# A hybrid decoder step on one core: norms and projections interleaved, free PSUM banks first, and eight idle matmuls ahead of the data

## The chip, the cores and the metric

One NeuronCore of a Trainium2 chip runs the whole program. The metric is the device time of one execution in microseconds (us); the profile shows one execution. TensorE is "PE" in the profile (its weight loads are "PEld"), VectorE "DVE", ScalarE "ACT", GpSimd "POOL", SyncE "SP"; a "q" behind an engine's name is its queue of DMA issues.

## The reference

One layer over 16 meta tokens, a prompt of 2048 and 64 sample tokens (8 sequences of 8), model width 1024. Cut to its frame:

```python
def layer(x):                       # x: tokens x 1024
    q, k, v, c, vm, o, i, f = split(x @ w_in)          # 512 128 128 512 512 512 4 4
    att = window_attention(q, k, v)                    # window 128, sinks, ALiBi
    h_m = mlstm(silu(conv4(c)), vm, i, f)              # 4 heads of 128, chunks of 128
    y = concat(head_norm(att), head_norm(sigmoid(o) * h_m))
    x1 = layer_norm(ALPHA * x + y @ w_out, ln1)
    ffn = (silu(x1 @ w_gate) * (x1 @ w_up)) @ w_down   # inner width 2816
    return layer_norm(ALPHA * x1 + ffn, ln2)           # and the caches and states
```

Matrix products must come out at float32 accuracy.

## The kernel before

Every large product is done in three passes (`mm3`, L125 to L127): each float32 operand is split into a high part, rounded to the fast matmul type (a cast, L113 on ScalarE, L115 on GpSimd, L117 on VectorE), and a low part, the difference (L122, on VectorE, now and then on GpSimd), and high x high, high x low and low x high are added up in PSUM. So each weight tile or activation tile that is loaded costs a DMA, a cast and a subtraction ahead of its first matmul.

A planner writes out the order of each engine's instructions when the kernel is built: it takes the instructions by their place in the Python code, and passes over those that are not ready by its own clock. On the chip every engine then keeps that order. `tc.issue_after(ins)` adds an edge: what is traced inside it on the engine of `ins` is put behind `ins` in that engine's order.

PSUM has two pools of banks: `pg` with three (`gps()`), `pb` with five (`bps()`).

The stages:

- First phase (to about 255 us): token tiles of 128 are projected onto v, the gates, vm and o with `w1a`. Tiles 0 and 1 run together, weight slice by weight slice as it arrives (`load_w1`), tile 0 in `gps`, tile 1 in `bps` banks. From tile 2 on each takes three banks in turn, from `gps` or `bps` by a counter `flip`. A tile's PSUM is emptied by VectorE and ScalarE (L273 to L298). `load_x` makes raw, high and low of a tile in buffers that share a tag. At the loop's thirteenth tile the code loads the first weights (`load_w`, one raw buffer `wbr`) and the first columns of x (`load_xg`) of the next phase; the planner hoists these.
- Second phase: q, k, c, the convolution and the maps of the mLSTM, by five groups of columns; the last group's three last projections (`late`) are left for the third phase.
- Third phase: five groups `g` of 384 to 440 tokens. For each: `out_proj` (eight steps `m` of 24 matmuls, each ended by the eviction L1091, ALPHA * z + projection), the layer norm `ln1`, gate and up (`gate_up`), and `down` in four slices, each of eight steps `m` ended by L1271. Attention and mLSTM of later tokens run between as background steps (`bg_step`, `pace`). `wnext` hands out weight tiles and loads three ahead.

The norms are Python generators; each `yield` gives the code around a place to put other work. `norm` (groups 1 to 4, and `ln2`): the mean by a matmul with `avg` (L1104), subtraction (L1108), squares (L1110), their sums (L1115), sums over partitions by matmuls (L453), 1/std on VectorE (`rsqrt`, L131 to L138) and its broadcast by matmuls (L465). `norm_early` (the first group's `ln1`, and the last group's `ln2_tail`) takes a provisional mean of the first four rows of tiles (`avg4`, L1128) while the rest is still being projected, and corrects it at the end: squares L1135, sums L1139, matmuls L1166 to L1171, 1/std, broadcast L1184. Then `scale` (L1205) multiplies, and ScalarE adds the bias (L1199 in the tail, L1214 and L1223 in `ln1`, whose low halves are L1221 on VectorE and L1224 on GpSimd).

The generators are stepped from outside: in the last slice of `down`, `ln1` of the next group is stepped twice at m = 0 and once at m = 1, 4 and 5; the tail's norm from m = 4 on; and in the first group `out_proj` steps it from m = 4 on, and the loop around `out_proj` runs it to its end before the `late` projections:

```python
        for _ in out_proj(z, y0, FF_GROUPS[0], lambda s: ln1(z, FF_GROUPS[0], s, x1, True, mark)):
            pass
        for m in late:
```

Of the kernel before, what the change touches and what calls it, by code (L numbers as in the profile page):

```python
# [16 lines left out]
D = 1024  # L17
# [27 lines left out]
CZ = 3  # L45

# [3 lines left out]
def tile_hymba(  # L50
# [42 lines left out]
    def constants():  # L93
        SP.dma_start(out=C, in_=cst)
        SP.dma_start(out=Q, in_=par)
        SP.dma_start(out=R, in_=rows.to_broadcast([128, 16]))
        V.memset(avg, 1.0 / D)
        V.memset(avg4, 2.0 / D)
        V.memset(one1, 1.0)
        V.tensor_copy(blk, C[:, C_BD:C_BD + 128])  # L100
# [40 lines left out]
    flip = [0]  # L141
# [43 lines left out]
    with ExitStack() as s1:  # L185
# [3 lines left out]
        def load_x(cols, parts=((0, KD),), eng="a"):  # L189
            raw = xp.tile([128, KD, 128], F32, tag="x", name="xr", bufs=6)  # L190
            hi = xp.tile([128, KD, 128], F32R, tag="x", name="xh", bufs=6)
            lo = xp.tile([128, KD, 128], F32R, tag="x", name="xl", bufs=6)
# [33 lines left out]

        x0, x1 = (load_x(tiles[i], ((0, 2), (2, KD)), "v") for i in range(2))
# [18 lines left out]
        for i in range(NCH + 1):  # L246
            if i == NCH - 4:
                with tc.issue_after(w1dma[0].ins):
                    for j in range(NEARLY):
                        load_w(j)  # L250
                    for k in range(KD):
                        load_xg(0, k)
# [45 lines left out]
            A.activation(out=o[0:n, 128:512], in_=pc[0:n, 0:384], func=AF.Tanh, scale=0.5)  # L298
# [712 lines left out]
    with ExitStack() as s2:  # L1011
# [34 lines left out]
        def wnext():  # L1046
            while len(ahead) < 3:
                t = next(wit, None)
                ahead.append(None if t is None else wtile(*t))
            return ahead.pop(0)  # L1050
# [33 lines left out]
        def out_proj(z, y, w, ln=None):  # L1084
            s = fp.tile([128, FW], F32, tag="zs", name="zs", bufs=2)
            for m in range(KD):
                h, l = wnext()
                p = gps()
                for k in range(KD):
                    mm3(p[:, 0:w], h[:, k, :], l[:, k, :], y[k][0][:, 0:w], y[k][1][:, 0:w], k == 0, k == KD - 1)  # L1090
                V.scalar_tensor_tensor(out=z[m][:, 0:w], in0=z[m][:, 0:w], scalar=ALPHA, in1=p[:, 0:w],  # L1091
                                       op0=ALU.mult, op1=ALU.add)
# [29 lines left out]
        def norm_early(z, w, s, pre):  # L1122
# [5 lines left out]
            PE.matmul(cm[:, 0:w], lhsT=avg4, rhs=s[:, 0:w], start=True, stop=True)  # L1128
            for k in (5, 6, 7):
# [30 lines left out]
            t = square(7)  # L1160
            parts = 3 if w % 3 == 0 and w <= 384 else 4
# [26 lines left out]
        def ln2_tail(z, g, s, w):  # L1188
            c0 = sum(FF_GROUPS[:g])
            ry = yield from norm_early(z, w, s, 1.0)  # L1190
            rs = ftmp()
            A.copy(rs[:, 0:w], ry[:, 0:w])
            for k in (6, 0, 1, 2, 7, 3, 4, 5):
                if k > 5:
                    G.tensor_tensor(out=z[k][:, 0:w], in0=z[k][:, 0:w], in1=rs[:, 0:w], op=ALU.mult)
                else:
                    scale(z, k, w, ry, Q_L2G)
            for k in (0, 1, 2, 6, 3, 4, 7, 5):
                A.activation(out=z[k][:, 0:w], in_=z[k][:, 0:w], func=AF.Identity, bias=Q[:, Q_L2B + k:Q_L2B + k + 1],  # L1199
                             scale=Q[:, Q_L2G + k:Q_L2G + k + 1] if k > 5 else 1.0)  # L1200
# [91 lines left out]
        for _ in out_proj(z, y0, FF_GROUPS[0], lambda s: ln1(z, FF_GROUPS[0], s, x1, True, mark)):  # L1292
            pass
        for m in late:
# [4 lines left out]
            out_q(None, p, m, cl, wl_)  # L1299
        ready[0] = T  # L1300
# [7 lines left out]
        for g in range(NG):  # L1308
# [4 lines left out]
            for s, n in enumerate(SLICES):  # L1313
# [21 lines left out]
                for m, _ in enumerate(down(z, hs, s, w, zs, 4 if last else KD)):  # L1335
                    if ln is not None and m in (0, 1, 4, 5):
# [3 lines left out]
                    if last and zs is not None and m >= 4:  # L1340
                        if m == 4:
# [130 lines left out]
```

## Time and profile before

| | us |
|---|---|
| median of 3 runs | 2491.41 |
| lowest and highest | 2490.56, 2494.92 |
| the profiled execution, its time | 2488.45 |
| its span on the core | 2486.7 |
| PE busy in it | 2438.5 |
| mean granted clock of PE | 0.993 |

A row of a timeline is: start, duration, engine, line, operation, output<-inputs, shape, count (merged rows), and in brackets the idle time before it and what ended that. A row of the stretches is: from:to, length, then busy time (and count) of PE, PEld, DVE, ACT, POOL, then PE's granted clock, the DMA share and GB/s. A matmul's duration holds its way through the array; matmuls in a row start closer together than they last. A row that begins with a line number gives minimum, median and maximum duration in ns and the first and last start.

### The profile page before, as it was taken

To read this page: it belongs to the slowest core of one execution; us is meant where nothing else is said; L and a number is where in the kernel's file an instruction comes from. 1 tells how busy PE (TensorE), PEld (TensorE's weight loads), DVE (VectorE), ACT (ScalarE), POOL (GpSimd) and SP (SyncE) were. 2 spreads that over 40 slices of the span, in tenths; PEclk is the share of its full clock that TensorE was granted. 3 is DMA by queue.
4 is the path that set the end of the run, shared out by engine and by line. 5 is a ranking of instruction groups with operands and counts; after the bars stand their busy time and mean duration, and the time that the engine had idled before them with its cause. 6 is when DMAs were issued, how large, how long until landed. Compare 5 with 4: busy or idle time off the path is not lost.

```text
span 2486.7 us, 35083 instructions
## 1 busy us (share of the span) xinstructions
PE 2438.5 (98%) x13189; PEld 2273.0 (91%) x13189; DVE 1535.3 (62%) x3195; ACT 965.3 (39%) x1752; POOL 311.6 (13%) x241
## 2 busy tenths in 40 slices
PE   8999999989999999999999999999999999999997
PEld 8999989889999998889999899989899999999997
DVE  5223577677877877757665886666765444764445
ACT  3112455545434445324443543343443323443332
POOL 1000000010000015110003300000410000420000
PEclk9999999999999999999999999999999999999998
DMA  7222534554444543554443354433344333343342
GB/s 236 91 91 76 174 117 127 171 174 139 152 139 127 170 135 110 181 153 136 127 132 116 118 182 122 139 113 116 102 143 130 120 111 119 102 145 113 119 127 78
DMA packets 188867, 327.89 MB, mean 132 GB/s; under 512 B 22546, under 2 KB 125034, under 8 KB 188682
## 3 DMA queue, kind: packets, MB, share of 16 engines
q1 hardware_dynamic: 170832, 294.40, 38.7%
q10 hardware_dynamic: 17866, 31.26, 3.4%
q8 instruction: 104, 1.70, 0.3%
q14 instruction: 65, 0.53, 0.1%
HBM read 281.59 MB, written 44.99 MB: 131 GB/s over the span
## 4 chain that ended last, share of the span: by engine, by line
PE 90%; DVE 4%; DMA 3%; ACT 1%; issue 1%; POOL 0%; ACTq 0%; SPq 0%; DVEq 0%; POOLq 0%
PE gps L125 25%; PE gps L126 25%; PE gps L127 25%; PE bps L125 2%; PE bps L127 2%; PE bps L126 2%; PE bps L516 2%; PE bps L552 1%; PE bps L545 1%; DVE w L122 1%; PE bps L658 1%; PE bps L685 1%; PE bps L675 1%; DMA w<-in_wd 1%; DMA w<-in_wg 1%
## 5 line engine op out<-in xcount | busy, mean ns | idle before, releaser
L127 PE MATMUL gps<-x,w 128*128 128x440 f32 (+4 forms) x2240 | 795.8, 356 | 4.3 <-POOL w L122 2.2
L126 PE MATMUL gps<-x,w 128*128 128x440 f32 (+4 forms) x2240 | 795.3, 356 | 0.0
L125 PE MATMUL gps<-x,w 128*128 128x440 f32 (+4 forms) x2240 | 790.0, 357 | 2.9 <-DVE z L1091 2.9
L113 ACT CAST w<-w 128x1024 fp32r<-128x1024 f32 (+2 forms) x423 | 400.5, 947 | 749.8 <-DMA w<-in_wd 261.1
L122 DVE TENSOR_TENSOR w<-w 128x1024 fp32r<-128x1024 f32 (+2 forms) x391 | 443.0, 1133 | 352.9 <-ACT w L113 163.7
L125 PEld LDWEIGHTS gps<-x,w 128*128 128x128 f32 x2240 | 420.5, 188 | 30.4 <-issue 5.4
L127 PEld LDWEIGHTS gps<-x,w 128*128 128x128 f32 x2240 | 420.9, 188 | 22.9 <-POOL w L122 3.7
L126 PEld LDWEIGHTS gps<-x,w 128*128 128x128 f32 x2240 | 421.1, 188 | 17.6 <-issue 0.2
L125 PE MATMUL gps<-hh,w 128*128 128x440 f32 (+2 forms) x880 | 314.6, 361 | 0.0
L127 PE MATMUL gps<-hh,w 128*128 128x440 f32 (+2 forms) x880 | 313.6, 358 | 0.0
L126 PE MATMUL gps<-hl,w 128*128 128x440 f32 (+2 forms) x880 | 312.9, 357 | 0.0
L122 POOL TENSOR_TENSOR w<-w 128x1024 fp32r<-128x1024 f32 x32 | 78.2, 2444 | 852.1 <-ACT w L113 611.5
L126 PEld LDWEIGHTS gps<-hl,w 128*128 128x128 f32 x880 | 166.5, 189 | 8.8 <-issue 2.3
L125 PEld LDWEIGHTS gps<-hh,w 128*128 128x128 f32 x880 | 166.1, 189 | 8.7 <-issue 1.7
L127 PEld LDWEIGHTS gps<-hh,w 128*128 128x128 f32 x880 | 166.2, 189 | 8.2 <-issue 1.1
L1271 DVE SCALAR_TENSOR_TENSOR z<-z,gps 128x440 f32<-128x440 f32 (+2 forms) x160 | 92.9, 589 | 57.7 <-PE gps L127 56.8
L113 ACT CAST hh<-hr 128x440 fp32r<-128x440 f32 (+2 forms) x110 | 60.0, 545 | 155.0 <-DVE hr L1257 154.9
L1257 DVE SCALAR_TENSOR_TENSOR hr<-ft,gps 128x440 f32<-128x440 f32 (+2 forms) x110 | 64.9, 590 | 81.7 <-PE gps L127 81.2
L1254 ACT ACTIVATE ft<-gps 128x440 f32<-128x440 f32 (+2 forms) x110 | 57.3, 521 | 106.3 <-PE gps L127 106.0
L122 DVE TENSOR_TENSOR hl<-hr,hh 128x440 fp32r<-128x440 f32 (+2 forms) x110 | 78.3, 712 | 27.2 <-ACT hh L113 26.7
L1255 DVE SCALAR_TENSOR_TENSOR ft<-ft,gps 128x440 f32<-128x440 f32 (+2 forms) x110 | 64.6, 588 | 39.5 <-ACT ft L1254 39.3
L126 PE MATMUL bps<-w1l,xh 128*128 128x384 f32 (+2 forms) x240 | 81.5, 339 | 0.0
(370 smaller groups left out, 3158.8 us busy)
## 6 DMA issues: line engine op xcount, KB each, us to landing
w<-in_wg SPq DMA_DIRECT2D x110, 512.0 KB, 3.5
w<-in_wu SPq DMA_DIRECT2D x110, 512.0 KB, 3.5
w<-in_wd SPq DMA_DIRECT2D x80, 384.0 KB, 3.1
w<-in_wd SPq DMA_DIRECT2D x80, 320.0 KB, 2.9
w<-in_wo SPq DMA_DIRECT2D x40, 512.0 KB, 3.7
FM<-ev ACTq DMA_DIRECT2D x52, 213.0 KB, 2.1
TM<-st ACTq DMA_DIRECT2D x16, 578.0 KB, 3.7
vmo<-TM SPq DMA_DIRECT2D x16, 514.0 KB, 3.5
```

The costliest lines, as they stand in the source:

```text
L113: A.copy(out, src)
L122: return veng.tensor_tensor(out=lo, in0=src, in1=hi.bitcast(F32), op=ALU.subtract)
L125: PE.matmul(out, lhsT=wh, rhs=xh, start=start, stop=False)
L126: PE.matmul(out, lhsT=wh, rhs=xl, start=False, stop=False)
L127: PE.matmul(out, lhsT=wl, rhs=xh, start=False, stop=stop)
L516: PE.matmul(s[g][:, j, 0:nk], lhsT=x[r, 2 * tt + j, :], rhs=y[r, 0:nk], start=(i == 0), stop=(i == 2))
L545: PE.transpose(pt[0:n, 128 * t:128 * t + 128], Pt[:, 4 * g + t, c0:c0 + n], ident)
L552: mm = PE.matmul(o[64 * g:64 * g + 64, :], lhsT=vt[0:n, j, 64 * g:64 * g + 64], rhs=ps[g][0:n], start=(j == 0), stop=(j == 1), skip_group_ ...
L1254: A.activation(out=t[:, 0:w], in_=pgt[:, 0:w], func=AF.Tanh, scale=0.5)
L1255: V.scalar_tensor_tensor(out=t[:, 0:w], in0=t[:, 0:w], scalar=1.0, in1=pgt[:, 0:w], op0=ALU.add, op1=ALU.mult)
L1257: V.scalar_tensor_tensor(out=hr[:, 0:w], in0=t[:, 0:w], scalar=0.5, in1=pu[:, 0:w], op0=ALU.mult, op1=ALU.mult)
L1271: V.scalar_tensor_tensor(out=zm, in0=zm, scalar=ALPHA if s == 0 else 1.0, in1=p[:, 0:w], op0=ALU.mult, op1=ALU.add)
```

## The change

- The memsets of `avg` and `avg4` move ahead of all loads, and eight matmuls of 128x128 on them are put into a bank that nothing reads (`WARM`).
- `flip` starts at 3, so tile 2 takes its three banks from `pb` first.
- `load_x` has seven buffers in place of six.
- The early `load_w` and `load_xg` get a second edge: their ScalarE work is put behind `evict`, ScalarE's last eviction of tile 1.
- `wnext(ins)`: in `out_proj` the splits of a tile that is newly loaded go behind the previous step's eviction on VectorE.
- `out_proj` starts `ln1` of the first group at m = 3 in place of 4; `norm_early` has three more yields (after the provisional mean, before the sums over partitions, before the broadcast); and the rest of that norm is stepped between the three `late` projections.
- The later `ln1` is stepped at m = 0, 0, 1, 3, 5 in place of 0, 0, 1, 4, 5; the tail's norm from m = 3 in place of 4.
- `ln2_tail` scales all eight tiles on VectorE and sends them in order; the copy of 1/std by ScalarE and two multiplications on GpSimd go.

```diff
-    flip = [0]
+    flip = [3]
...
-            raw = xp.tile([128, KD, 128], F32, tag="x", name="xr", bufs=6)
+            raw = xp.tile([128, KD, 128], F32, tag="x", name="xr", bufs=7)
...
+        V.memset(avg, 1.0 / D)
+        V.memset(avg4, 2.0 / D)
+        p = bps()
+        for _ in range(WARM):
+            PE.matmul(p[:, 0:128], lhsT=avg, rhs=avg4, start=True, stop=True)
...
-                with tc.issue_after(w1dma[0].ins):
+                with tc.issue_after(w1dma[0].ins), tc.issue_after(evict):
                     for j in range(NEARLY):
                         load_w(j)
...
+            if i == 1:
+                evict = a.ins
...
+                else:
+                    with tc.issue_after(ins):
+                        ahead.append(wtile(*t))
...
+            ins = None
             for m in range(KD):
-                h, l = wnext()
+                h, l = wnext(ins)
...
-                elif m == 4:
-                    ln = ln(s)
-                if ln is not None and m >= 4:
+                if ln is not None and m >= 3:
+                    if m == 3:
+                        ln = ln(s)
                     next(ln)
...
             PE.matmul(cm[:, 0:w], lhsT=avg4, rhs=s[:, 0:w], start=True, stop=True)
+            yield
...
             t = square(7)
+            yield
...
+            yield
             rb = bps()
...
-            rs = ftmp()
-            A.copy(rs[:, 0:w], ry[:, 0:w])
-            for k in (6, 0, 1, 2, 7, 3, 4, 5):
-                if k > 5:
-                    G.tensor_tensor(out=z[k][:, 0:w], in0=z[k][:, 0:w], in1=rs[:, 0:w], op=ALU.mult)
-                else:
-                    scale(z, k, w, ry, Q_L2G)
-            for k in (0, 1, 2, 6, 3, 4, 7, 5):
+            for k in range(KD):
+                scale(z, k, w, ry, Q_L2G)
                 A.activation(out=z[k][:, 0:w], in_=z[k][:, 0:w], func=AF.Identity,
                              bias=Q[:, Q_L2B + k:Q_L2B + k + 1])
...
+        first = out_proj(z, y0, FF_GROUPS[0], lambda s: ln1(z, FF_GROUPS[0], s, x1, True, mark))
         for m in late:
...
             out_q(None, p, m, cl, wl_)
+            next(first, None)
+        for _ in first:
+            pass
...
-                    if ln is not None and m in (0, 1, 4, 5):
+                    if ln is not None and m in (0, 1, 3, 5):
...
-                    if last and zs is not None and m >= 4:
-                        if m == 4:
+                    if last and zs is not None and m >= 3:
+                        if m == 3:
                             pend = ln2_tail(z, g, zs, w)
```

More of the change, by code (lines that the diff above doesn't have):

```diff
@@ L45 @@
 CZ = 3
+WARM = 8
 @with_exitstack
@@ L96, in constants @@
         SP.dma_start(out=R, in_=rows.to_broadcast([128, 16]))
-        V.memset(avg, 1.0 / D)
-        V.memset(avg4, 2.0 / D)
         V.memset(one1, 1.0)
@@ L189, in load_x @@
         def load_x(cols, parts=((0, KD),), eng="a"):
-            raw = xp.tile([128, KD, 128], F32, tag="x", name="xr", bufs=6)
-            hi = xp.tile([128, KD, 128], F32R, tag="x", name="xh", bufs=6)
-            lo = xp.tile([128, KD, 128], F32R, tag="x", name="xl", bufs=6)
+            raw = xp.tile([128, KD, 128], F32, tag="x", name="xr", bufs=7)
+            hi = xp.tile([128, KD, 128], F32R, tag="x", name="xh", bufs=7)
+            lo = xp.tile([128, KD, 128], F32R, tag="x", name="xl", bufs=7)
             n = sum(w for _, w in cols)
@@ L297, in tile_hymba @@
             A.activation(out=o[0:n, 0:128], in_=pbk[0:n, 256:384], func=AF.Tanh, scale=0.5)
-            A.activation(out=o[0:n, 128:512], in_=pc[0:n, 0:384], func=AF.Tanh, scale=0.5)
+            a = A.activation(out=o[0:n, 128:512], in_=pc[0:n, 0:384], func=AF.Tanh, scale=0.5)
+            if i == 1:
+                evict = a.ins
             G.tensor_scalar(out=o[0:n], in0=o[0:n], scalar1=0.5, scalar2=0.5, op0=ALU.mult, op1=ALU.add)
@@ L1044, in tile_hymba, with wnext @@
         ahead = []
-        def wnext():
+        def wnext(ins=None):
             while len(ahead) < 3:
                 t = next(wit, None)
-                ahead.append(None if t is None else wtile(*t))
+                if t is None:
+                    ahead.append(None)
+                elif ins is None:
+                    ahead.append(wtile(*t))
+                else:
+                    with tc.issue_after(ins):
+                        ahead.append(wtile(*t))
             return ahead.pop(0)
@@ L1090, in out_proj @@
                     mm3(p[:, 0:w], h[:, k, :], l[:, k, :], y[k][0][:, 0:w], y[k][1][:, 0:w], k == 0, k == KD - 1)
-                V.scalar_tensor_tensor(out=z[m][:, 0:w], in0=z[m][:, 0:w], scalar=ALPHA, in1=p[:, 0:w],
-                                       op0=ALU.mult, op1=ALU.add)
+                ins = V.scalar_tensor_tensor(out=z[m][:, 0:w], in0=z[m][:, 0:w], scalar=ALPHA, in1=p[:, 0:w],
+                                             op0=ALU.mult, op1=ALU.add).ins
                 if ln is None or m < 4:
                     add_to(s, z, m, w, G if ln is None else V)
-                elif m == 4:
-                    ln = ln(s)
-                if ln is not None and m >= 4:
+                if ln is not None and m >= 3:
+                    if m == 3:
+                        ln = ln(s)
                     next(ln)
@@ L1291, in tile_hymba @@
         mark = {7: None}
-        for _ in out_proj(z, y0, FF_GROUPS[0], lambda s: ln1(z, FF_GROUPS[0], s, x1, True, mark)):
-            pass
+        first = out_proj(z, y0, FF_GROUPS[0], lambda s: ln1(z, FF_GROUPS[0], s, x1, True, mark))
         for m in late:
```

4 lines of the change are left out of this document (2 added, 2 removed).

## Prediction

> **What bounds the kernel now.** I read the page first, then TensorE's waits, then the granted clock by stretches, and last the timelines around each wait.
>
> ```profile
> span 2486.7 us, 35083 instructions
> PE 2438.5 (98%) x13189; PEld 2273.0 (91%) x13189; DVE 1535.3 (62%) x3195; ACT 965.3 (39%) x1752; POOL 311.6 (13%) x241
> ```
>
> TensorE is busy for all but 48.2 us. The change takes away no matmul, so all that it can win lies in those 48 us, in matmuls that run at a lowered clock, and behind the last matmul. The waits say where the idle time is:
>
> ```profile
> PE gps L465 <- DVE rs L138: 7.3, 4, 3.5
> PE bps L1166 <- DVE ft L1139: 6.3, 2, 3.5
> PE bps L1184 <- DVE rs L138: 5.7, 2, 2.9
> PE gps L125 <- DVE w1h L117: 4.2, 1, 4.2
> PE gps L125 <- DVE z L1091: 2.9, 4, 0.9
> PE gps L125 <- ACT st L298: 2.5, 1, 2.5
> PE gps L127 <- POOL w L122: 2.2, 3, 1.1
> PE gps L127 <- DVE w L122: 2.0, 3, 0.9
> ```
>
> The columns are total us, times, longest. L465 is the broadcast of 1/std in `norm`, L1166 and L1184 are the two sums of `norm_early` (the first group and the tail), L1091 a PSUM bank that waits for its eviction in `out_proj`, L298 the eviction of tile 0, and the L127 rows are weights whose low half comes late. The L125 wait for w1h is the start, before any data. Idle time also lowers the clock; the fourth figure from the right is what was granted:
>
> ```profile
> 33.00:42.00 9.00, 6.51 (x28) 6.20 (x28) 6.71 (x13) 4.65 (x10) 3.32 (x4) 0.81 0.88 280
> 534.00:551.00 17.00, 10.70 (x47) 9.51 (x46) 15.53 (x39) 5.35 (x9) 1.04 (x1) 0.70 0.19 61
> 954.00:964.00 10.00, 6.46 (x32) 6.15 (x31) 8.53 (x19) 4.43 (x8) 4.44 (x3) 0.83 0.16 52
> 1785.00:1793.00 8.00, 5.65 (x24) 5.14 (x24) 7.25 (x11) 3.65 (x6) 4.29 (x3) 0.79 0.21 66
> ```
>
> 9.0 x 0.19, 10.0 x 0.17 and 8.0 x 0.21 are each 1.7 us of lost clock. 17.0 x 0.30 is 5.1 us, a half clock for 10.2 us, of which 2.8 us were idle anyway: 3.7 us lost.
>
> **The change, part by part.** The sum is made against the profiled execution (span 2486.7, time 2488.45) and moved to the median of the runs, 2491.41, which lies 2.96 us above it.
>
> *Eight idle matmuls at the start: 0.*
>
> ```profile
> 9.26 0.52 PE L125 MATMUL bps<-w1h,xh 128*128 128x384 f32 x1
> ...
> 10.69 1.36 DVE L122 TENSOR_TENSOR w1l<-w1r,w1h 128x1160 fp32r<-128x1160 f32 x1
> ...
> 12.10 0.45 PE L126 MATMUL gps<-w1l,xh 128*128 128x392 f32 x1
> 12.39 0.34 PE L127 MATMUL gps<-w1h,xl 128*128 128x392 f32 x1
> 12.56 0.34 PE L126 MATMUL gps<-w1l,xh 128*128 128x384 f32 x1
> ```
>
> Early matmuls take 0.52 us, from 12.39 on they take 0.34 and follow each other in 0.17. So the start runs slow. But the matmul at 12.10 begins when VectorE ends the low half of the second weight slice (10.69 + 1.36 = 12.05), and that hangs on loads and casts. A faster start only waits longer there. The trace has no idle matmul; the nearest row is L1184 below (three fp32 matmuls of 128x128 in 1.65 us at the lowered clock): eight are about 4.4 us, from 1.2 (after two memsets) to 5.6, past the first real matmul at 4.18. Bounds: 0.3 won, 1.0 lost; I take 0.
> The Trainium skill, "TensorE: Matmul & The Clock Gate", Part 1, says that TensorE starts throttled and is released after about 3.4 us of activity; the trace agrees that the start is slow. By that rule alone the idle matmuls would release it before the data come, and as an estimate from the Trainium skill's 3.4 us some 2 us of slow start would be won; the sum would be that much lower.
>
> *First phase, free banks: 4.2 won.*
>
> ```profile
> 30.96 0.33 SPq L172 DMA_DIRECT2D wbr<-in_w1b  x1
> ...
> 31.97 0.55 SPq L197 DMA_DIRECT2D xr<-in_xT  x1
> ...
> 33.06 1.22 DVE L122 TENSOR_TENSOR xl<-xr,xh 128x1024 fp32r<-128x1024 f32 x1
> ...
> 36.01 0.45 PE L125 MATMUL gps<-w1h,xh 128*128 128x392 f32 x1 [2.49 <-ACT st L298]
> ```
>
> Tile 2 waits 2.5 us for tile 0's bank, and its own low half (33.06) also came late, for want of a buffer. With `flip` at 3 its first two parts go into `pb` banks that are free (the idle matmuls' bank included), 48 matmuls x 0.175 (the 0.17 to 0.18 between the matmuls from 12.39) = 8.4 us of work from 33.5, where tile 2 began to wait, until 41.9; the evictions of tiles 0 and 1 are done well before. The seventh buffer lets the low half be made early. Holding ScalarE's casts behind tile 1's eviction holds more than casts: `wbr` has one buffer, so SyncE's next `wbr` load stays in its queue, and with it tile 3's `xr`, queued two places behind. If the first cast starts at 36, when tile 2's bank came free, instead of before 30.96, that load slips by some 7 us to 39; landing and two casts (six us, an estimate from its own 1.2 for a split) bring it to about 45, and tile 3 starts at 33.5 + 72 x 0.175 = 46.1. It is covered, with 1 us left. Won: 2.5 idle and 1.7 clock. Bounds 0 to 4.2.
>
> *The first group's passage: 9.0 won.*
>
> ```profile
> 538.40 0.83 PE L1166 MATMUL bps<-avg,ft 128*128 128x1 f32 x6 [3.48 <-DVE ft L1139]
> ...
> 545.73 1.65 PE L1184 MATMUL bps<-C,rs 128*128 128x128 f32 x6 [2.82 <-DVE rs L138]
> 550.00:562.00 12.00, 12.00 (x64) 11.63 (x62) 7.10 (x10) 9.52 (x17) 4.86 (x4) 1.00 0.38 123
> 562.24 0.98 PE L516 MATMUL bps<-kt,qt 64*128 64x256 f32 x12
> ...
> 564.50 0.42 PE L125 MATMUL gps<-x,w 128*128 128x384 f32 x1
> L1224 POOL TENSOR_TENSOR x<-z,x x4: 1023/1170/1544, 550.0 to 558.5; 128x384 fp32r<-128x384 f32 x4
> ```
>
> Now the norm stands alone between `out_proj` (ends at 535) and the three `late` projections, then 2.3 us of background work, then the first gate at 564.50. The change puts the projections between the norm's steps. The row by stretch has 64 matmuls in 12.0 us, 0.188 each, so one projection is 24 x 0.188 = 4.5. New order: projection to 539.5; sums, due at 538.4 before, so no wait, 2.2 us (18 one-column matmuls at the 0.1 of L453's rows below, and 0.4 for the wide one), to 541.7; projection to 546.2, over a 1/std that took 2.8; broadcast 0.8, half of its 1.65 at the lowered clock, to 547.0; projection to 551.5; background to 553.8. The cover moved to the front is gone behind: x1's last low half was done at 558.5 + 1.0 = 559.5, 12.1 after the broadcast ended (545.73 + 1.65 = 547.4), so it will be done at 559.1. The first gate needs it 7 x 0.53 + 0.35 into its run, at 557.9: a new wait of 1.2. It starts in effect at 555.0 instead of 564.5; I take 9.0 of the 9.5. Bounds: 4 (x1 delays each step) to 11.7 (both idles, the clock, and most of the 2.0 us of L127 waits for VectorE, which lie in this `out_proj`).
>
> *Sums one step earlier in the later norms (m 3 for m 4): 0.9 lost.*
>
> ```profile
> 947.32 2.15 DVE L1115 TENSOR_TENSOR ft<-ft 128x440 f32<-128x440 f32 x2
> 949.66 1.61 PE L453 MATMUL gps<-avg,ft 128*110 128x1 f32 x16
> ...
> 1365.95 2.07 DVE L1115 TENSOR_TENSOR ft<-ft 128x440 f32<-128x440 f32 x2
> 1369.44 1.62 PE L453 MATMUL gps<-avg,ft 128*110 128x1 f32 x16
> ```
>
> 1/std then gets two `down` steps instead of one and L465's 7.3 us go, with 3.4 of clock. What is late next is the sums' input. A step is 18 matmuls: 3.2 us at 0.175, 3.6 at the 0.2 of 440 columns. One step earlier the sums of the first two norms stand at 946.5 and 1365.8; VectorE ends their inputs at 949.5 and 1368.0. That is 3.0 and 2.2 of waiting, and the same reading gives 2.0 and 1.0 in the other two: 8.2 in place of 7.3. Idle of 2.5 us lowered the clock in the first phase, so I count two lowered stretches again. Bounds: 10.7 won (the order written out holds the sums back until they are ready) to 4.3 lost (all four waits lower the clock, 0.9 and twice 1.7).
>
> *`out_proj` evictions ahead of later weights: 2.6 won.*
>
> ```profile
> 1735.14 1.22 DVE L122 TENSOR_TENSOR w<-w 128x1024 fp32r<-128x1024 f32 x1 [6.93 <-issue]
> 1736.28 1.13 DVE L1091 SCALAR_TENSOR_TENSOR z<-z,gps 128x440 f32<-128x440 f32 x2
> ```
>
> VectorE sat idle for 6.9 us before a weight split while evictions that were ready stood behind it. With the edge the first eviction goes ahead, and the 2.9 us of L1091 go but for some tenths, since the split is then still the next weight's last step. Queued behind a held split are later splits and the x casts; TensorE waits for them. Bounds 0 to 2.9, apart from the rival below.
>
> *Tail: 1.8 won.*
>
> ```profile
> 2452.88 0.58 DVE L1082 TENSOR_TENSOR zs<-zs,z 128x408 f32<-128x408 f32 x1
> ...
> 2457.92 0.51 PE L1128 MATMUL bps<-zs,avg 128*128 128x408 f32 x1
> ...
> 2477.80 0.50 ACT L1192 COPY ft<-bps 128x408 f32<-128x408 f32 x1 [10.37 <-PE bps L1184]
> 2478.33 3.39 DVE L1205 SCALAR_TENSOR_TENSOR z<-z,Q,bps 128x408 f32<-128x408 f32 x6 [0.82 <-ACT ft L1192]
> ...
> 2479.00 4.50 ACT L1199 ACTIVATE z<-z,Q 128x408 f32<-128x408 f32 x8 [0.70 <-DVE z L1205]
> ```
>
> The copy goes and VectorE scales all eight, 0.55 apart, from about 2477.75: the last ends at 2482.25, ScalarE's last 0.6 behind it at 2482.9, against 2479.00 + 4.50 = 2483.5 now: 0.6 won. The mean's matmul ran 4.5 us after its input; a step earlier, all of the variance moves up and up to 2.4 of the 2.8 us before L1166 could go. Whether the order written out moves it is open: it already stood later than the code asks. I take half, 1.2. Bounds 0.6 to 3.0.
>
> Sum: 0 + 4.2 + 9.0 - 0.9 + 2.6 + 1.8 = 16.7 won. 2491.4 - 16.7 = 2474.7, so 2475; the profiled execution 2471.8.
>
> **Rivals.**
> 1. The later norms come clean: sums are placed where their input is ready, and 10.7 is won in place of 0.9 lost. For it: L453 shows no wait today. Against: L465 was placed 3.5 us too early, so the written order trusts VectorE too much. 2474.7 - 11.6 = 2463.
> 2. x1 becomes the wait in the first group. Its chain is 12.1 us and only 4.5 of projection and 4.2 of gate surely lie beside it: 3.4 of idle and 1.7 of clock where I took 1.2, and the casts of the first gate weights stand behind it. That is near the lower bound of 4 in place of 9.0: 2480.
> 3. Slower: in `out_proj` a split now stands behind an eviction that waits for TensorE, so each weight comes late. The price of such a wait is in the L127 row for VectorE, up to 0.9. Over 40 steps it is 36 us: 2475 + 36 = 2511. It turns the result from 16.7 / 40 = 0.42 us a step. Against: the edge is to the step before, and three weights are held ahead.
> 4. The written order changes elsewhere and gives the gain back: within 5 us of before, about 2489. For it: nearly every wait above is between work that the planner believed ready.
> 5. The start counts: the idle matmuls bring the clock up before the data, and the written order puts the split of 10.69 sooner, so that the slow third of the start, where 0.52 us goes to what takes 0.34 later, is won: of the 5.6 us from 4.2 to 9.8 about 5.6 x (1 - 0.34 / 0.52) = 1.9, 2473. Against: the 12.10 row. The Trainium skill's release after activity, cited above, is this rival.
>
> **How the numbers follow.** Chances: forecast 0.45 (2469 to 2479), rival 1 0.22, rival 2 0.15 (2480 to 2485), rival 3 0.06, rival 4 0.07, rival 5 0.05. 0.2% is 5 us, about what a measurement of this kernel tells from no change. Faster: 0.45 + 0.22 + 0.15 + 0.05 = 0.87; same 0.07; slower 0.06. The range leaves out rivals 3 and 4 and the ends of 1: 2460 to 2485.
>
> **What would show it.** Right: no wait for L298 and a clock of 1.00 from 33 to 42; no L1166 or L1184 wait in the first group; L1091 nearly gone; new waits at L453 in the later norms; the last ScalarE row 0.6 us nearer to the broadcast. Wrong: L465 and L453 both free (rival 1), waits of the first gate for x1 over 2 us (rival 2), many L127 waits for w in `out_proj` (rival 3).

## The result, and the profile after

| | before | after |
|---|---|---|
| median, us | 2490.98 (4 runs, 2486.93 to 2494.92) | 2469.72 (4 runs, 2469.47 to 2476.45) |
| profiled execution, its time and span | 2488.45, 2486.7 | 2476.45, 2474.6 |
| granted clock in it | 0.993 | 0.994 |

The ratio is 0.9919, 95% interval 0.9903 to 0.9935: 20 us won, between 16 and 24. Of the four runs after, three lie within 0.4 us of 2469.6; the profiled one is the fourth, 6.7 us above them. So the profile after shows less than the change wins; the repeat in experiment 1 has a profile of the usual kind, and is read beside it. The line numbers move with the change: L122 is now L121 (a split's low half), L125 to L127 are L124 to L126 (the three passes), L453 and L465 are L460 and L472, L1091 is L1105, L1166 and L1184 are L1182 and L1201, L1271 is L1282.

The head of the page after:

```profile
span 2474.6 us, 35105 instructions
...
PE 2438.2 (99%) x13205; PEld 2273.4 (92%) x13205; DVE 1531.3 (62%) x3197; ACT 963.1 (39%) x1751; POOL 314.6 (13%) x239
```

TensorE's waits after (us in total, times, longest):

```profile
PE bps L1201 <- DVE rs L137: 4.4, 2, 2.9
PE gps L472 <- DVE rs L137: 4.1, 3, 3.6
PE gps L126 <- DVE w L121: 3.5, 6, 0.9
PE bps L1182 <- DVE ft L1154: 2.8, 1, 2.8
PE gps L126 <- POOL w L121: 2.8, 4, 1.0
```

Against the rows of before: the waits for st L298 (2.5) and for the banks of L1091 (2.9) are gone; the sums of `norm_early` wait once, not twice (6.3 to 2.8); their broadcast waits 1.4 us in the passage and 2.9 in the tail (5.7 to 4.4); 1/std in the later norms went from 7.3 to 4.1, all but 0.5 of it in the first of them; and the late low halves grew, from 2.0 to 3.5 on VectorE and from 2.2 to 2.8 on GpSimd. The granted clock (the third figure from the right; the prediction calls it the fourth) in stretches, the first two and last two of them those of before:

```profile
33.00:42.00 9.00, 9.00 (x53) 8.99 (x52) 7.28 (x18) 5.63 (x11) 2.17 (x2) 1.00 0.61 188
534.00:551.00 17.00, 15.56 (x96) 14.24 (x95) 14.93 (x36) 8.67 (x13) 1.01 (x1) 1.00 0.37 117
...
946.77:950.18 3.41, 3.07 (x12) 3.08 (x13) 1.24 (x5) 0.28 (x1) 0.99 (x1) 0.50 0.00 0
950.18:953.60 3.42, 3.42 (x12) 3.42 (x12) 3.42 (x7) 3.39 (x6) 0.77 (x1) 0.50 0.00 0
954.00:964.00 10.00, 10.00 (x55) 9.61 (x54) 6.98 (x8) 8.22 (x13) 7.51 (x5) 1.00 0.33 106
1785.00:1793.00 8.00, 8.00 (x42) 7.48 (x41) 7.67 (x8) 6.40 (x12) 7.70 (x5) 1.00 0.29 98
```

Of the four lowered stretches of before that the prediction shows, three are gone and the one at the first later norm is longer: 6.8 us at half clock in place of 3.4.

### The profile page after: what moved, and what is told of

It is laid out like the page before. It is cut to its first block, busy times and chain, and to the rows that moved or that the text cites. A ratio compares the mean times of both kernels' runs of the same rounds, so it can differ in the third digit from the quotient of the medians.

```text
span 2474.6 us, 35105 instructions
## 1 busy us (share of the span) xinstructions
PE 2438.2 (99%) x13205; PEld 2273.4 (92%) x13205; DVE 1531.3 (62%) x3197; ACT 963.1 (39%) x1751; POOL 314.6 (13%) x239
## 4 chain that ended last, share of the span: by engine, by line
PE 93%; DVE 3%; DMA 2%; ACT 1%; issue 0%; POOL 0%; SPq 0%; ACTq 0%; DVEq 0%
PE gps L124 26%; PE gps L126 26%; PE gps L125 26%; PE bps L124 2%; PE bps L125 2%; PE bps L126 2%; PE bps L523 2%; PE bps L559 1%; PE bps L552 1%; PE bps L665 1%; PE bps L692 1%; PE bps L682 1%; DVE w L121 1%; PE bps L693 1%; DMA w<-in_wo 0%
## 5 line engine op out<-in xcount | busy, mean ns | idle before, releaser
L126 PE MATMUL gps<-x,w 128*128 128x440 f32 (+4 forms) x2240 | 796.7, 356 | 6.4 <-DVE w L121 3.5
L125 PE MATMUL gps<-x,w 128*128 128x440 f32 (+4 forms) x2240 | 794.1, 356 | 0.0
L124 PE MATMUL gps<-x,w 128*128 128x440 f32 (+4 forms) x2240 | 790.4, 357 | 0.0
L121 DVE TENSOR_TENSOR w<-w 128x1024 fp32r<-128x1024 f32 (+2 forms) x391 | 441.0, 1128 | 326.4 <-ACT w L112 168.0
L126 PEld LDWEIGHTS gps<-x,w 128*128 128x128 f32 x2240 | 420.9, 188 | 26.7 <-DVE w L121 6.0
L124 PEld LDWEIGHTS gps<-x,w 128*128 128x128 f32 x2240 | 420.5, 188 | 26.7 <-issue 5.4
L125 PEld LDWEIGHTS gps<-x,w 128*128 128x128 f32 x2240 | 421.2, 188 | 17.7 <-issue 0.2
L124 PE MATMUL gps<-hh,w 128*128 128x440 f32 (+2 forms) x880 | 314.3, 361 | 0.0
L126 PE MATMUL gps<-hh,w 128*128 128x440 f32 (+2 forms) x880 | 313.5, 358 | 0.0
L125 PE MATMUL gps<-hl,w 128*128 128x440 f32 (+2 forms) x880 | 312.6, 357 | 0.0
L121 POOL TENSOR_TENSOR w<-w 128x1024 fp32r<-128x1024 f32 x32 | 77.6, 2425 | 846.5 <-ACT w L112 654.1
L125 PEld LDWEIGHTS gps<-hl,w 128*128 128x128 f32 x880 | 166.2, 189 | 8.7 <-issue 2.3
L124 PEld LDWEIGHTS gps<-hh,w 128*128 128x128 f32 x880 | 166.0, 189 | 8.6 <-issue 2.1
L126 PEld LDWEIGHTS gps<-hh,w 128*128 128x128 f32 x880 | 166.0, 189 | 8.2 <-issue 1.5
L1282 DVE SCALAR_TENSOR_TENSOR z<-z,gps 128x440 f32<-128x440 f32 (+2 forms) x160 | 92.9, 589 | 56.6 <-PE gps L126 55.9
L121 DVE TENSOR_TENSOR hl<-hr,hh 128x440 fp32r<-128x440 f32 (+2 forms) x110 | 81.3, 739 | 27.2 <-ACT hh L112 26.9
L125 PE MATMUL bps<-w1l,xh 128*128 128x384 f32 (+3 forms) x264 | 89.7, 340 | 0.0
```

The source lines that it names most:

```text
L121: return veng.tensor_tensor(out=lo, in0=src, in1=hi.bitcast(F32), op=ALU.subtract)
L124: PE.matmul(out, lhsT=wh, rhs=xh, start=start, stop=False)
L125: PE.matmul(out, lhsT=wh, rhs=xl, start=False, stop=False)
L126: PE.matmul(out, lhsT=wl, rhs=xh, start=False, stop=stop)
L1282: V.scalar_tensor_tensor(out=zm, in0=zm, scalar=ALPHA if s == 0 else 1.0, in1=p[:, 0:w], op0=ALU.mult, op1=ALU.add)
```

## The experiments

The kernels ran in four groups (1 to 4, 5 to 8, 9 to 11, 12) beside 26, 29, 11 and 9 runs of the kernel before; each ratio is to the runs of the same chip. A run's span and mean clock are known, so an upper bound of its loss by the clock can be worked out, (1 - clock) x span. Over the 26 runs of before in the first group it is 20.4 us of 2491, over the five of the repeat 9.4 of 2469: 11 of the 22 us between them. It is an upper bound because a lowered clock costs nothing while TensorE has nothing to run, as in most of the tail. Counted only where TensorE was busy, the loss is 10.6 us in the profile of before and 3.5 in that of the repeat, 7 of the 18 us between these two. So a third to a half of the gain is clock, and the rest is waits.

**1. The changed kernel again.**

> The changed kernel once more, nothing altered, as the yardstick of this study. Theory: three of its first four times lie within 0.4 us of 2469.6 and the profiled one at 2476.5, and that one shows a stretch of 6.83 us at a lowered clock (946.8 to 953.6) where one of 3.41 would do and 21 us of it at the end; so I expect about 2470 us, 0.8% below the kernel before, with single runs up to 7 us apart, and a profile whose lowered stretches lie elsewhere or are fewer. Rival: the four times were luck and the kernel is at 2476.

Measured: 2470.66 (2469.21 to 2474.62, 5 runs) against 2492.70; ratio 0.9912 (0.9898 to 0.9926). The span of the profiled run is 2468.9, 5.7 us under the other profile, and its only lowered stretch after the start is the one at the end. The difference lies in the first later norm. Timelines of the first profile after, VectorE, GpSimd and TensorE around that norm's 1/std:

```profile
943.93 2.19 DVE L137 SCALAR_TENSOR_TENSOR rs<-rs 110x4 f32<-110x4 f32 x1
...
943.73 2.37 POOL L121 TENSOR_TENSOR w<-w 128x1024 fp32r<-128x1024 f32 x1 [1.05 <-ACT w L112]
...
947.11 2.04 PE L472 MATMUL gps<-C,rs 110*128 110x110 f32 x8 [3.60 <-DVE rs L137]
```

and the same of the repeat:

```profile
944.13 0.16 DVE L137 SCALAR_TENSOR_TENSOR rs<-rs 110x4 f32<-110x4 f32 x1
...
944.38 2.37 POOL L121 TENSOR_TENSOR w<-w 128x1024 fp32r<-128x1024 f32 x1 [2.43 <-ACT w L112]
...
944.35 1.14 PE L472 MATMUL gps<-C,rs 110*128 110x110 f32 x8 [1.54 <-DVE rs L137]
```

A VectorE instruction on 110x4 elements that takes 0.16 us takes 2.19 when GpSimd's split of a weight runs beside it: it ends when the split ends, at 946.1. In the repeat the split starts 0.1 us after the chain is done. That makes 2.06 us more of wait, and 6.8 us at half clock, 3.4: 5.5 of the 5.7. The other profiles bear it out: in the fourteen traces of this case 29 VectorE steps of a 1/std took 1.5 us or more, and each of them ended 15 to 27 ns behind a GpSimd instruction that ran beside it. The Trainium skill, "SBUF — State Buffer", section "SBUF: two separate sides", says that a VectorE operation with two SBUF inputs and a GpSimd operation hold a shared port as an exclusive lock; these rows agree. The profile of before has this collision too, in the first later norm and in the third:

```profile
954.53 2.34 POOL L122 TENSOR_TENSOR w<-w 128x1024 fp32r<-128x1024 f32 x1 [0.95 <-PE gps L127]
954.63 2.25 DVE L137 SCALAR_TENSOR_TENSOR rs<-rs 110x4 f32<-110x4 f32 x1
...
1785.05 2.34 POOL L122 TENSOR_TENSOR w<-w 128x1024 fp32r<-128x1024 f32 x1 [1.50 <-PE gps L126]
1785.18 2.23 DVE L138 SCALAR_TENSOR_TENSOR rs<-rs 110x4 f32<-110x4 f32 x1
```

These two norms hold 5.9 of the 7.3 us at L465, so a good part of that wait was never a matter of the step alone that asks for the sums. The prediction does not have this.

**2 to 7. Each part alone, on the kernel before.**

First phase:

```diff
-    flip = [0]
+    flip = [3]
...
-  ... tag="x", name="xr", bufs=6)      (and xh, xl)
+  ... tag="x", name="xr", bufs=7)
...
-                with tc.issue_after(w1dma[0].ins):
+                with tc.issue_after(w1dma[0].ins), tc.issue_after(evict):
```

> The kernel before with the first-phase part alone (flip at 3, seventh buffer, first cast of the w1b tiles behind tile 1's last eviction), without the idle matmuls. From the two traces: this part moved the end of the first phase 4.2 us forward (2.49 idle at tile 2's bank and 1.7 of lowered clock), so 2491 - 4.2 = 2486.8, with no wait of TensorE for st and a clock of 1.00 from 33 to 42 us. Rival: the gain is taken up again by the attention work that follows, which is ordered by due times, and the time stays within 1 us of the kernel before.

Passage (with the three new yields of `norm_early`, which keeps its old steps in the tail):

```diff
+                if ln is not None and m >= 3:
+                    if m == 3:
+                        ln = ln(s)
...
+            next(first, None)        # behind each of the late projections
```

> The kernel before with the first group's passage alone (sums one step earlier, the three late projections between the norm's steps; the tail's norm is left as it was). The prediction's term is 9.0 us won; the two traces of the whole change give 7.1 (the marker at 724.49 moved by 10.95, of which 3.86 came from before). Theory: 7 us won, 2484, with a wait of about 1.4 us left at the 1/std, because a weight split of 1.23 us stands inside that chain on VectorE. Rival: without the earlier first phase the planner orders the splits otherwise, the chain is covered, and the full 9.0 is won, 2482; or x1 becomes the wait of the first gate and it is 4, 2487.

Later norms:

```diff
-                    if ln is not None and m in (0, 1, 4, 5):
+                    if ln is not None and m in (0, 1, 3, 5):
```

> The kernel before with the later norms' step alone (third call at down step 3 in place of 4). The prediction's term is 0.9 us lost, by new waits of the sums for their input (3.0, 2.2, 2.0, 1.0) in place of 7.3 at the 1/std. The trace of the whole change shows no such wait: the order written out held 14 of the 16 sum matmuls back to where they stood, and the wait for 1/std went from 7.3 to 4.1, the one in the first later norm staying at 3.6. So theory: 3 to 5 us won (3.2 of waits and one lowered stretch of 1.7), 2487, and no wait at the sums. Rival, the prediction's: 2492 with waits at the sums of 1 to 3 us.

`out_proj`, the eviction ahead of the next weight:

```diff
-                h, l = wnext()
+                h, l = wnext(ins)
```

> The kernel before with the edge in out_proj alone (a new weight's casts and split behind the eviction of the step before). The prediction's term is 2.6 us won. The traces of the whole change: the 2.9 us of bank waits are gone, but the waits for a weight's low half grew from 2.0 to 3.5 us on VectorE and from 2.2 to 2.8 on GpSimd. Theory: 0.8 us won, 2490, with that exchange to be seen. Rival, the prediction's: 2.6 won; rival 3 of the prediction: each weight late by up to 0.9, 2520.

Tail (with the same yields for the tail alone, and its norm stepped from m = 3):

```diff
-            rs = ftmp()
-            A.copy(rs[:, 0:w], ry[:, 0:w])
...
+            for k in range(KD):
+                scale(z, k, w, ry, Q_L2G)
```

> The kernel before with the tail alone (VectorE scales all eight rows, no copy to ScalarE, sums of the last norm asked for a step earlier). The prediction's term is 1.8 us: 0.6 by the scaling and 1.2 by an earlier mean. The traces of the whole change show the mean's matmul in its old place, the two waits unchanged (2.84 and 2.92) and 0.77 us less from the last matmul to the end. Theory: 0.7 us won. Rival: 1.8 or more, if the mean moves here.

Idle matmuls:

```diff
+        p = bps()
+        for _ in range(8):
+            PE.matmul(p[:, 0:128], lhsT=avg, rhs=avg4, start=True, stop=True)
```

> The kernel before with the eight idle matmuls at the start alone (and the two memsets that feed them moved there). The prediction's term is 0, bounds 0.3 won and 1.0 lost. In the trace of the whole change they end at 4.91, the clock is released at 4.72 instead of 10.2, falls at 8.13 after a wait of 1.39 us for the first weights, and rises again at 11.54; the low half of the second slice comes 0.76 later. Theory: within 1 us of the kernel before, 0 to 0.8 lost. Rival 5 of the prediction: 1.9 won by the warm start.

Measured, us (the ratio's interval in us of 2492 in the last column):

| part | median, runs | ratio | won |
|---|---|---|---|
| first phase | 2490.95, 12 | 0.9993 (0.9982 to 1.0004) | 1.7 (4.5 to -1.0) |
| passage | 2485.58, 9 | 0.9972 (0.9962 to 0.9982) | 7.0 (9.5 to 4.5) |
| later norms | 2490.56, 12 | 0.9993 (0.9983 to 1.0003) | 1.7 (4.2 to -0.7) |
| evictions | 2489.35, 11 | 0.9994 (0.9984 to 1.0004) | 1.5 (4.0 to -1.0) |
| tail | 2491.42, 12 | 0.9995 (0.9986 to 1.0003) | 1.2 (3.5 to -0.7) |
| idle matmuls | 2493.75, 12 | 0.9994 (0.9984 to 1.0005) | 1.5 (4.0 to -1.2) |

The ratio is not that of the two medians; for the idle matmuls the medians even point the other way. By time alone only the passage is shown: the 4.2 us expected of the first phase and the 3 to 5 expected of the later norms lie at the far end of their intervals. The traces say more. With the first phase alone its last matmul ends 4.5 us earlier than in the kernel before and there is no wait for st; but that profile has a lowered stretch of 6.8 us from 722.8 that before does not have, 6.8 in place of 3.4 at the first later norm (from 958.4), and longer waits for P (3.2 us in place of 0.3, and 1.6 more at one instruction), and its span is 7 us longer than the one of before. With the later norms alone L453 does not wait, and L465 waits less, though the long one stays; what is gone is mostly the third norm's, 0.27 in place of 2.35, without the collision:

```profile
PE gps L465 <- DVE rs L138: 4.6, 4, 3.8
```

With the evictions alone the bank waits (2.9) are gone, and the late weights take most of it back:

```profile
PE gps L127 <- DVE w L122: 3.7, 6, 0.9
PE gps L127 <- POOL w L122: 2.7, 4, 1.0
```

That is 2.9 against 1.7 + 0.5: 0.7 us. The third norm's collision and its wait are gone in this profile too, so that no single part can be said to remove them. With the tail alone the mean's matmul stays where it was and the waits before the sums and the broadcast are as before. The parts sum to 0.0059 of the time, 15 us, the whole to 0.0088, 22; with intervals of 0.001 on each of six parts and 0.0014 on the whole, some 0.0028 together, a difference of 0.0029 does not firmly show that they differ.

**8. The changed kernel without the idle matmuls.**

```diff
-        for _ in range(WARM):
-            PE.matmul(p[:, 0:128], lhsT=avg, rhs=avg4, start=True, stop=True)
```

> The changed kernel without the eight idle matmuls, everything else as in it. The same question from the other side. Theory: the matmuls buy nothing, so this is the changed kernel's 2469.6 less 0 to 0.8, and the second slice's low half is at 12.1 again. Rival: they are worth 1.9 us and this is 2471.5. A third possibility: they set where the clock's windows fall later on, and this kernel differs by some us with no cause in the first phase; then its lowered stretches lie elsewhere than the changed kernel's.

Measured: 2476.78 (2474.96 to 2482.13, 6 runs), ratio 0.9940 (0.9928 to 0.9952): 6 us more than experiment 1, where the theory had 0 to 0.8 less and the rival 1.9 more. The third possibility allowed for some us, but by where the clock's steps fall. Yet its first phase ends 3.8 us earlier than that of before, as in the profile after (3.7) and within half a us of the repeat (4.3). The two profiles are 5.9 us apart, and nearly all of it stands at the first later norm: a wait of 3.75 and 6.8 us of half clock, which makes 5.6 us more than in the repeat, by the collision above.

**9 and 10. That split on VectorE, with and without the idle matmuls.** Two weights of 423 (the first gate weight of the second and the fourth group) are split on VectorE.

```diff
-  ... G if n == 8 and (wcount[0] % WP == 0 or
+  ... G if n == 8 and (wcount[0] % WP == 0 and wcount[0] not in (96, 264) or
```

> The changed kernel with two weight splits (the first gate weight of the second and of the fourth group of columns) on VectorE instead of GpSimd, nothing else. In the changed kernel's profiled run a VectorE instruction of the first later norm's 1/std takes 2.19 us instead of 0.16 beside GpSimd's split (943.73, 2.37 long); TensorE waits 3.60 and the clock is halved for 6.8 us. In the repeat the same split begins at 944.38, after the chain: the wait is 1.54, no lowered stretch, and the run is 5.8 us shorter. Theory: whether that split falls into the chain or behind it is what makes most of the scatter of the changed kernel; without it the runs are at 2470 and none is at 2475 or above, with a wait of about 1.5 for the 1/std there (or up to 2.8, if VectorE now runs the split of 1.22 inside the chain, which costs 1.2 to 3). Rival: the scatter is of another origin, and runs at 2475 stay.

> The changed kernel without the eight idle matmuls, and with the same two splits on VectorE. All runs without the idle matmuls were at 2475 to 2482, and the profiled one had the long wait (3.75) and 6.8 us of half clock at the first later norm, but lay only 0.5 us behind the repeat of the changed kernel at 250 us. Theory: the 6 us between the kernels with and without idle matmuls are the collision with GpSimd's split, not the start; with the split moved they differ by 0.5 to 2 us, this one at 2471 to 2472. Rival: the idle matmuls are worth 6 us by themselves, and this stays at 2476.

Measured: 2476.72 with the idle matmuls (2475.18 to 2477.44, 5 runs; ratio 0.9927, 0.9912 to 0.9943) and 2475.75 without (2471.09 to 2477.20, 6 runs; 0.9923, 0.9908 to 0.9938). My theory for 9 fell: VectorE now puts the split inside the chain itself, one instruction before its end, where it takes 1.96 us; I had named that proviso, but with a wait of 2.8 at most. VectorE in experiment 9:

```profile
946.13 0.15 DVE L136 SCALAR_TENSOR_TENSOR rs<-rs 110x4 f32<-110x4 f32 x1
946.47 1.96 DVE L121 TENSOR_TENSOR w<-w 128x1024 fp32r<-128x1024 f32 x1 [0.19 <-ACT w L112]
948.35 0.15 DVE L137 SCALAR_TENSOR_TENSOR rs<-rs 110x4 f32<-110x4 f32 x1
```

So TensorE waits 3.54 there in 9 and 3.37 in 10. It still answers the question of 8: with the long wait in both kernels, the idle matmuls make no difference that shows (1.0 us, the wrong way, with overlapping runs). By their times, all six runs of 8 (2475 and more) and two of the nine of the changed kernel (2474.6 and 2476.5) seem to have the collision; only the profiled ones show it, and why the two kernels differ in this is not settled. Where the split met the chain (the profile after and 8), the cast before it began 3.6 and 4.0 us after the weight's load was issued; in the repeat it was 4.9.

Experiment 10's profile also has a wait of 3.37 that lowered nothing: between the start and the tail its clock stays at full. The stretches are cut at the clock's own steps, first for 10, then for 9:

```profile
941.40:944.80 3.40, 1.62 (x10) 1.30 (x8) 3.11 (x12) 1.05 (x1) 1.18 (x2) 1.00 0.27 43
944.80:948.20 3.40, 1.81 (x13) 1.81 (x14) 2.16 (x4) 1.05 (x1) 1.52 (x1) 1.00 0.30 119
948.20:951.60 3.40, 3.40 (x22) 3.40 (x21) 3.40 (x7) 3.25 (x6) 1.14 (x1) 1.00 0.00 0
```

```profile
943.10:946.50 3.40, 1.91 (x11) 1.59 (x10) 2.90 (x14) 1.04 (x1) 1.18 (x2) 1.00 0.31 67
946.50:949.90 3.40, 1.35 (x10) 1.35 (x11) 2.17 (x3) 1.04 (x1) 0.84 (x1) 1.00 0.34 133
949.90:953.30 3.40, 3.40 (x12) 3.40 (x12) 3.40 (x7) 2.83 (x5) 0.84 (x1) 0.50 0.00 0
```

In all fourteen traces of this case every change of the clock lies on a grid of 3.413 us, which starts anywhere. In 10 the wait fell across two steps of the grid, with 1.8 and 1.6 us of idle time in them (length less busy time), and nothing happened; in 9 one step held 2.05, and the next ran at half clock.

**11. The chains kept clear.** Every weight split that is traced after a norm's 1/std is put behind it on VectorE, the two splits of 9 too; in the tail two late squares are added on GpSimd, and their sum goes into the variance as an operand of its own.

```diff
+            with tc.issue_after(root_[0]) if root_[0] else ExitStack():
+                split("a", hi[:, 0:n], lo[:, 0:n], raw[:, 0:n], ...)
...
+                add(G, q0, q0, square(6))
+            PE.matmul(vd[0:n, c:c + 1], lhsT=q0[:, n * c:n * c + n], rhs=one, ...)
```

> The changed kernel with the two splits on VectorE, with every weight split that is asked for after a norm's 1/std ordered behind that chain on VectorE, and in the tail two of the three late sums of squares on GpSimd, whose running sum goes into TensorE's variance as an operand of its own. Theory: the wait of 1.45 in the first group's passage goes (two splits of 1.23 stand inside that chain), the one in the first later norm falls to 1.5 or less, and in the tail the wait of 2.84 before the sums goes, with some of the lowered clock behind it: 1.4 + 0 to 2 + 3 less, 2465. Rivals: the splits held back make the first gate's weights late (a new wait for a low half of up to 1.2); GpSimd's sums in the tail, 1.07 each, hold up VectorE's, and the wait in the tail falls by 1 only: 2469.

Measured: 2483.64 (2481.09 to 2485.15, 6 runs), ratio 0.9955 (0.9939 to 0.9970). The waits that it was made for are gone or short (the passage's broadcast does not wait, the tail's sums wait 0.67), and it is 11 us slower than the changed kernel by the ratios of 1 and 11 (13 by the medians, which stand in different groups). The largest of TensorE's waits:

```profile
PE gps L126 <- DVE w L121: 12.7, 16, 2.8
```

Sixteen late low halves in place of the repeat's six (3.6 us): in all four later norms the splits that were held back were the next to be used. The rival that I had priced at up to 1.2 us cost 9 us of waits.

**12. Three splits only.** The edges stay on the first two gate weights of the first group and the first of the second; in the tail one square is added on GpSimd, and one is an operand of its own.

```diff
+            with tc.issue_after(root_[0]) if wcount[0] in (12, 13, 96) else ExitStack():
```

> The changed kernel with three weight splits only (the first two gate weights of the first group of columns, and the first of the second group, which is moved to VectorE) ordered behind the 1/std before them, and in the tail one late sum of squares on GpSimd and one as an operand of TensorE's own, so that VectorE's last sums meet one GpSimd instruction fewer. In the kernel with all splits held, the wait of 1.45 in the first group's passage and that of 2.84 in the tail were gone and last down matmul to end fell from 21.2 to 20.0 us, but each of the later norms then waited for a late weight, and 10 us more were lost from 940 us on. Theory: without those edges that loss goes, and 1.4 (passage), 0 to 2 (first later norm) and 1.2 to 2 (tail) remain: 2466 to 2468, with a spread of a few us by the clock. Rival: the split held behind the first later norm still makes that gate late, or any new edge moves the rest of the written order, and it is no better than the changed kernel's 2470. Clock: in the tail TensorE then has no idle time before the sums, only some 2.7 us of one-column matmuls; if the clock falls there all the same, such matmuls do not hold it up.

Measured: 2471.43 (2469.77 to 2471.96, 5 runs), ratio 0.9914 (0.9898 to 0.9930): as fast as the changed kernel, not faster. In its profile the passage has no wait at the broadcast, the first later norm waits 1.28, the tail's sums do not wait, and from the last `down` matmul to the end it is 18.9 us against 21.7 in the repeat. But that matmul stands 2.0 us later than in the repeat: the planner laid the background work out anew, and waits of 0.3 to 1.7 us stand there that were not there or were shorter (P for L830 2.3 in place of 1.3, the normalised queries of L610 1.4 in place of 1.1, L756 0.7). The gain at three places was turned into small waits elsewhere. On the clock it gave an answer, in the tail. The stretches, and TensorE's one-column matmuls in the second of them:

```profile
2445.60:2449.00 3.40, 3.40 (x20) 3.40 (x19) 3.40 (x5) 1.98 (x5) 3.03 (x3) 1.00 0.00 0
2449.10:2452.50 3.40, 3.40 (x32) 2.89 (x30) 1.76 (x5) 0.54 (x1) 0.00 (x0) 1.00 0.00 0
2452.50:2455.00 2.50, 2.27 (x14) 2.18 (x13) 2.15 (x5) 0.00 (x0) 0.00 (x0) 0.50 0.00 0
...
2449.28 0.88 PE L1188 MATMUL bps<-avg,ft 128*102 128x1 f32 x8
2450.02 0.86 PE L1192 MATMUL bps<-avg,ft 128*102 128x1 f32 x8
2450.74 0.86 PE L1192 MATMUL bps<-avg,sq 128*102 128x1 f32 x8
```

From 2449.1 to 2452.5 TensorE is never idle, and the clock still falls at 2452.5. What it runs there is mostly matmuls with one column, 24 records from 2449.28 on and some of the next eight.

No version that beats the changed kernel came out.

## Why the prediction was right, and where its sum was not

The predicted 2475 lies 5 us above the measured 2469.7, inside the range. Starts of the same matmul in the traces put the change in four places (us against the profile of before; the last matmul of the in-projections at 489.87, the first and the last of `down` at 619.37 and 2465.88, the end 2486.66):

| place | predicted | profile after | repeat |
|---|---|---|---|
| up to the end of the in-projections | -4.2 | -3.9 | -4.8 |
| passage, to the first `down` | -9.0 | -7.5 | -7.5 |
| later norms and `out_proj`, to the last `down` | +0.9 - 2.6 | -1.9 | -6.4 |
| behind it | -1.8 | +1.3 | +1.0 |
| sum | -16.7 | -12.0 | -17.8 |

The repeat's sum agrees with the forecast to 1.1 us, but as a sum of errors that cancel: 6.2 too much (1.5 in the passage, 1.9 in `out_proj`, 2.8 behind the last `down`) and 7.2 too little (6.6 in the later norms, 0.6 up to the in-projections). So far the closeness is luck.

- *Idle matmuls, 0:* right. In the profile after they end at 4.91, and the clock is released at 4.72 instead of 10.2; then the wait for the first weights comes, and the clock is lost again for the step from 8.13:

```profile
1.31:4.72 3.41, 3.41 (x17) 3.41 (x17) 1.59 (x5) 0.70 (x1) 0.00 (x0) 1.00 0.79 208
4.72:8.13 3.41, 1.64 (x8) 0.98 (x7) 1.36 (x3) 0.83 (x1) 0.00 (x0) 1.00 1.03 342
8.13:11.54 3.41, 3.41 (x12) 3.41 (x12) 3.03 (x6) 1.16 (x1) 0.03 (x1) 0.50 1.07 401
```

  (The record of the clock begins at 4.72; the first row's 1.00 is no measurement.) In the repeat the same matmuls did not release it before 10.2; the step from 3.4 to 6.8 had 0.6 us of idle time. In the six profiles with idle matmuls (these two and experiments 7, 9, 11 and 12) the release comes at 4.4 to 10.2, in the eight without at 9.4 to 12.7; experiments 7, 9 and 10 show no gain by it. Rival 5 has the release and not the gain. The Trainium skill, "TensorE: Matmul & The Clock Gate", Part 1, which I drew on for 3.4 us of activity, also says there that the window runs free of the kernel's start; both traces agree with that, and it is the half of the rule that I left out.
- *First phase, 4.2:* right, in size and place: 3.7 to 4.7 at its last matmul in five traces (the profile after, experiments 1, 2, 8 and 12); in the five kernels without this part (experiments 3 to 7) it lies between 1.5 earlier and 2.1 later. The step that I feared for, tile 3's load behind the held casts, was covered.
- *First group's passage, 9.0:* mis-sized, 7.5. The wait of 1.2 for x1 did not come. What came was a step that I had counted as covered: the 1/std "that took 2.8" lay under a projection, but two weight splits were put into the chain, since VectorE now had ready work there. VectorE and TensorE in the profile after:

```profile
538.98 1.21 DVE L121 TENSOR_TENSOR w<-w 128x1024 fp32r<-128x1024 f32 x1
...
542.88 1.23 DVE L121 TENSOR_TENSOR w<-w 128x1024 fp32r<-128x1024 f32 x1 [0.64 <-PE bps L125]
...
544.43 0.93 PE L1201 MATMUL bps<-C,rs 128*128 128x128 f32 x6 [1.44 <-DVE rs L137]
```

  Experiments 11 and 12 hold these two splits back, and the 1.44 go; the passage is then 8.6 us shorter than before's in 12, but 7.4 in 11. I had read the chain's length off a stretch in which VectorE had nothing else to do.
- *Later norms, 0.9 lost:* wrong in sign. The 8.2 us of new waits that I put at the sums do not exist: the planner moved 2 of the 16 records one step up and kept 14 behind their input, as rival 1 has it. TensorE in the profile after:

```profile
935.49 0.26 PE L460 MATMUL gps<-avg,ft 128*110 128x1 f32 x2
938.84 1.42 PE L460 MATMUL gps<-avg,ft 128*110 128x1 f32 x14
```

  Nor did the 14 have to move by a step: in the first later norm they stand where they stood, in the last three 4 or 5 `down` matmuls earlier. There the chain now starts 0.3 us after the last of them began, in place of 1.0 to 1.8, and L472 waits 0.26, 0.26 and not at all, where it waited up to 2.4. The 2.4 was the collision with GpSimd's split in the third norm, so that part of the gain is not the step's alone. Rival 1's 10.7 was not reached either, because of the first later norm: its wait is 3.60 with the collision, and 1.54 without it in the repeat. With 0.7 for the evictions taken off the table's row, the gain is 1.2 to 5.7, by which of the two profiles of experiment 1 one gets. That rival was worth more than the 0.22 I gave it.
- *Evictions, 2.6:* 0.7. The bank waits went as said; "but for some tenths" was the error. The weight behind the eviction is late by 0.3 to 0.5 in four more steps of `out_proj`: rival 3's mechanism, in four steps, not 40.
- *Tail, 1.8:* the scaling gave what was forecast, 0.6 from the end of the last matmul to ScalarE's last row (5.8 to 5.2), and 0.67 to the end of the program (8.95 to 8.28; the 0.77 that experiment 6 expects is too much). The mean did not move, so the 1.2 that I took as half of 2.4 are 0. Yet the stretch is a us longer than in the profile of before, because the clock there fell 5.3 us after the last `down` matmul began, and here 2.9 to 3.6 after it. In the five kernels above whose tail is that of before, this stretch is 0.4 to 1.7 longer than in that profile, too, with the clock falling at 3.5 to 4.9; in experiments 8 to 10, which have the new tail, it falls at 4.5 to 4.8 and the stretch is within 0.2 of that profile's.
- *The profile to the median:* the profile of before (2488.45) was 3.6 to 6.1 us under the medians of the four groups of later runs (2492.0 to 2494.6), so that the sum, right against the profile, is short against the medians.

## What to carry to other kernels

Before a stall is taken out by putting work beside a short chain of dependent instructions, ask what else becomes ready on that chain's engine: here weight splits of 1.2 us were put into chains of 0.16 us steps, and one on GpSimd held up VectorE as long as one on VectorE itself. Holding them back by an edge did not pay here: three splits came out even, and all of them lost 11 us, because the held result was the next to be used. And when a kernel's runs differ by some us, cut the granted clock at its own steps before taking any difference for an effect: here a third to a half of the gain was clock, and so was a good part of the scatter. Over the 75 runs of before, the spread (one standard deviation) falls from 3.0 us to 2.0 when each span is multiplied by its mean clock.

## What the runs showed of the hardware

- The clock is set in steps of 3.413 us on a grid that starts anywhere. In the fourteen traces, 34 steps at full clock held 1.9 us or more of idle time, and half clock followed every one of them. Between 1.5 and 1.9 both happened (1.6 at 489 us in experiment 9 and 1.77 in the start of the profile after lowered it, 1.68 in experiment 12 and 1.8 in experiment 10 did not). With 1.5 or less it fell after five steps: three that held one-column matmuls (0 in experiment 12, 0.33 in 11, 1.26 in the tail of before), and two near 490 us (1.07 in experiment 3, 1.24 in 11), whose cause is open. So idle time of 0.56 of a step was always enough here; what decides below that is not shown. The Trainium skill, "TensorE: Matmul & The Clock Gate", section "Why this matters for your kernels", asks for no idle gaps over about 3 us; here gaps of 2.3 to 2.5 lowered the clock, and one of 3.37 did not.
- Matmuls with one column seem not to hold the clock: it fell after a step without any idle time, of which they filled some 2.2 us without a break (experiment 12), and after one with 0.33 us of idle time (11). With 1.6 us of them in a step, as in the sums of the later norms of before, it stayed.
- One VectorE instruction of 0.16 us took 2.19 beside a GpSimd split of 2.37, on fp32 tiles in SBUF, and so did others, 29 of 1.5 us or more in the fourteen traces.
